# Expert weights held as two neighbouring rows per partition, with the matching operands' columns stepped by two

## The chip, the core and the metric

The kernel runs on one core of a Trainium2 chip. Its time is the device time of one execution in microseconds (us), the median of three runs. The engines that the text names are TensorE (PE, with its weight loads listed apart as PEld), VectorE (DVE), ScalarE (ACT), GpSimd (POOL) and SyncE (SP), whose queue issues nearly all loads. The core's 16 DMA engines move the bytes.

## What is computed

Two blocks of a network follow each other on 256 tokens of 1024 channels, all in float32. The first has a mixer (attention and a gated network), a norm, and then routed experts: each token goes to four of 32 experts. The change touches the experts alone; cut to what matters, the reference has for a group of tokens `xb` and an expert `e`:

```python
logits = (xt @ w_router + b_router).astype(jnp.float32)
top_vals, top_idx = lax.top_k(logits, TOP_K)
gates = jax.nn.softmax(top_vals, axis=-1).astype(x.dtype)
...
def expert_block(args):
    xb, e = args
    gt = jnp.minimum(xb @ w_gate[e] + b_gate[e], SWIGLU_LIMIT)
    up = jnp.clip(xb @ w_up[e] + b_up[e], -SWIGLU_LIMIT, SWIGLU_LIMIT)
    hid = gt * jax.nn.sigmoid(SWIGLU_ALPHA * gt) * (up + 1.0)
    return hid @ w_down[e] + b_down[e]
...
out = jnp.zeros((T + 1, D), x.dtype).at[row_tok].add(y_rows * row_gate[:, None])[:T]
```

Every expert has three matrices of 1024 x 1024 in float32, 4 MiB each, and all of them are read once: 384 MiB. The second block (another mixer and a network with a convolution) follows.

## The kernel before

**The experts' weights.** Each matrix is cut into four pieces of 256 rows, 1 MiB, that lie in memory in one stretch. `expert_pieces` lists them in the order of need: gate and up of expert e, then down of expert e-1. A piece lands in a tile of [128 partitions, 2048 floats]. Row 128 * k + p of the piece goes to half k of partition p, so a partition holds two rows that are 128 rows apart, each a run of 4 KB. `fetch` issues the DMAs on SP's queue (line 188, in `piece`); the first 18 pieces are issued in the first part (line 1251, in `pump`). There are 18 slots, used in turn: a piece can be issued when the products on the one that is 18 pieces ahead of it in its slot are done.

**The products.** Every expert has 64 slots for its tokens. For a pair of experts `gather` multiplies the tokens' rows `h` (as stationary operand, 128 columns at a time) with a matrix of zeros and ones: `xg` then holds, for each chunk k of 128 channels, the channels by partition and the slots by column. `product` sums over the chunks k: `xg[:, k]` is the stationary operand and half k % 2 of piece k // 2 is the moving one, so channel and weight row must agree in each partition. `hidden_t` turns the hidden values `sg` in four transposes to `hidT`, which plays the same part for the down product. `scatter` adds the results to the tokens' sums.

**The order.** It is written out by hand in the loop over experts at the end of `moe`: gate and up of e, the gather for the next pair (in every second e), down of e-1, the transposes. Behind expert 15 (`REST`) stands a loop, `overflow`, for experts with more than 64 tokens; its count is read at run time. It has weight loads of its own, [128, 1024], in the tile `wx`. `self.mm` is line 77 and `self.tr` line 81 for all products and transposes, so the groups of the profile are told apart by their tiles: `g`, `u`, `y` for the products with gate, up and down; `tr` and `sc` with `oh,h` for the gather; `tr<-ident,sg` for the transposes of `hidden_t`.

Of the kernel before, what the change touches and what calls it, by code (L numbers as in the profile page):

```python
# [30 lines left out]
# slots for pieces of weights: what each holds in the first part (raw pieces, their parts, the rest)  # L31
SLOTS_A = "r8 c1 c0 c2 c3 c4".split()
SLOTS_B = "r0 r1 r2 r3 r4 r5 r6 r7 h0 h1 h2 h3".split()
# the expert before whose successor the tokens that found no slot have their turn
# [25 lines left out]
class Net:  # L60
# [22 lines left out]
    def rsqrt_steps(self, pool, v, n, add=0.0, mul=1.0, floor=None, out=None):  # L83
        """Steps of 1/sqrt(max(mul * v, floor) + add) of small float32 tiles [128, n], by Newton steps from an
        integer guess. Halving and negating, as the steps want it, keeps the bits but for exponent and sign."""
# [26 lines left out]
    @staticmethod  # L112
    def alternate(*chains):
        """Emits chains of steps in turn, so that none waits for its own last step alone."""
        todo = list(chains)
        while todo:
            for g in list(todo):
                if next(g, todo) is todo:
                    todo.remove(g)
# [7 lines left out]
    def run(self):  # L127
# [20 lines left out]
        # for the experts' routing: ones; what comes before, in bits; the slots' numbers  # L148
# [33 lines left out]
    def piece(self, src, name="w"):  # L182
        """One weight piece: src is a list of (view of the tile, dram ap)."""
        pool, i = self.rings[self.turn % len(self.rings)]
        self.turn += 1
        t = pool.tile([128, 2048], F32, tag=i, name=self.nm(name))
        for view, ap in src(t):
            self.nc.sync.dma_start(view, ap)
        return t

    def front(self, fctx):
# [18 lines left out]
        # slots for weights: pieces as they come, their two parts, and what the output projection no longer needs  # L210
# [15 lines left out]
        # inputs, in the order in which they are needed; then the first experts' weights  # L226
# [8 lines left out]
        def add(src, *keys):  # L235
            """A piece and its halves, of columns for two keys, else of rows."""
            k, n = src.shape[1] , src.shape[2]
            spec.append((k, src))
            for x, key in enumerate(keys * (2 if len(keys) == 1 else 1)):
                halves.append((key, len(spec) - 1, (lambda t, x=x: t[:, :, x * n // 2:(x + 1) * n // 2]) if len(keys) == 2  # L240
                               else (lambda t, x=x: t[:, x * k // 2:(x + 1) * k // 2, :])))
# [49 lines left out]
        # masks  # L291
# [12 lines left out]
        # identities below one another  # L304
# [33 lines left out]
        def through(*names):  # L338
            """These slots go on to the experts' weights."""
            self.raw_slots += [slot[i] for i in names]  # L340
            self.pump()

        def channels(key):
            """[channel, token] of 128 columns."""
# [7 lines left out]
        # k transposed (each kv head in both halves), v by tokens, q transposed  # L352
# [8 lines left out]
        # spatial weights transposed  # L361
# [16 lines left out]
        # scores: groups of (query tile, chunks), each with one bank for either head of the chunks  # L378
# [39 lines left out]
        def trp(i):  # L418
            """Transposed, over what it came from."""
# [20 lines left out]
        # gated mlp: its second part by tokens  # L440
# [71 lines left out]
        # output projection, residual, layer norm, router  # L512
        wr, ln1g, ln1b = L["wr"], L["ln1g"], L["ln1b"]
        lst = [f2.tile([128, 4, 6], F32, tag="lst", name=self.nm("lst")) for _ in range(NT)]
        # the row that the norm's bias adds to the logits
        def by_experts(rhs, n, E):
            """[(part of the sum, expert), n] of the router's products."""
# [19 lines left out]
        def norm(t):  # L537
            """Steps of the norm, up to the last factor and the bias, and of that factor."""
# [72 lines left out]
    def split_biases(self, bf):  # L611
        """Biases of gate and up in three bf16 parts that add up to them exactly, by expert; in steps."""
# [13 lines left out]

    def expert_pieces(self):
        """The experts' weights as they are needed: gate and up, then down of the expert before."""
        r = []
        for e in range(NE + 1):  # L630
            for x, names in ((e, ("w_gate", "w_up")), (e - 1, ("w_down",)), (e, ("w_down",))):
                if x in range(NE) and (len(names) == 2 or (x == e) == (x == REST)):
                    for nme in names:
                        v = self.a[nme][0, x].rearrange("(k p) c -> p k c", p=128)
                        r += [((x, nme, i), v[:, 2 * i:2 * i + 2, :]) for i in range(4)]
        return r

    def fetch(self, n):
        """Loads the experts' weights up to the n-th piece."""
# [4 lines left out]
    def moe(self, mctx):  # L644
# [52 lines left out]
        def gather(b):  # L697
            xg[b] = m2.tile([128, KC, EB * CAP], F32, tag="xg", bufs=1, name=self.nm("xg"))
            for c0 in range(0, KC, 4):
                p = bank(*(("sc", 2) if c0 else ("tr", 1)), [128, 4, EB * CAP])  # L700
                for c in range(4):
                    for t in range(NT):
                        self.mm(p[:, c, :], self.h[:, t, (c0 + c) * 128:(c0 + c + 1) * 128],
# [7 lines left out]
        def scatter(yv, og_t, rows=128, sums=None):  # L711
            """With sums, these start with the sum so far and are left as they are."""
# [10 lines left out]
        def product(p, lhs, w, start):  # L723
            """p[(half, token)] (+)= lhs(k) @ w(k), either half of the columns in a half of the array."""
# [5 lines left out]
        def gated_slots(og, n):  # L730
            """[(expert, slot), token] of the gates of the slots' tokens."""
# [7 lines left out]
        def gates_of(b):  # L739
            """The gates in their slots; then, as a step of its own, turned."""  # L740
# [16 lines left out]
        def hidden_t(sg):  # L757
            hidT = m2.tile([128, 4, 2, CAP], F32, tag="hidT", bufs=1, name=self.nm("hidT"))
            p = bank("tr", 1, [128, 4, 128])
            for j in range(4):  # L760
                self.tr(p[:, j, :], sg[:, j * 128:(j + 1) * 128])
# [23 lines left out]
        def flush(sums=None):  # L785
            """Adds the last pair's products to the sum."""
# [3 lines left out]
        # experts with more tokens than slots: the rest, in further groups of slots  # L790
# [5 lines left out]
        def overflow_lists():  # L796
            """Entry i: the i-th group of slots past the first that some expert needs."""
# [24 lines left out]
            # first slot of the group: CAP * (1 + (entry - expert) / NE)  # L822
# [19 lines left out]
        def overflow():  # L842
            n = nc.values_load(lists["num"][0:1, 0:1], min_val=0, max_val=NL - 1)
            with tc.For_i(0, n, 1) as i:
# [15 lines left out]
                for k in range(KC):  # L860
                    for t in range(NT):
                        self.mm(p[:, k, :], self.h[:, t, k * 128:(k + 1) * 128], oh[:, t], start=t == 0, stop=t == NT - 1)
                nc.vector.tensor_copy(xo, p)

                def weights(nme):
                    def f(k):
                        w = m2.tile([128, D], F32, tag="wx", bufs=1, name=self.nm("wx"))
                        nc.sync.dma_start(w, a[nme][0, bass.ds(e, 1), k * 128:(k + 1) * 128, :].rearrange("o p c -> (o p) c"))
# [27 lines left out]
        def start_sum():  # L896
            # residual and the gated biases of the last product start the sum
# [17 lines left out]
        def ahead(n):  # L915
            """Before the work on the next n pieces: those that their forerunners have left slots for."""
# [44 lines left out]
        # the last sums start from what there is  # L961
# [5 lines left out]
        # the norms' weights, in slots that are through; the first weights of the mixer; then the last sums  # L967
# [15 lines left out]

    def late_consts(self, scratch):
        """Small inputs and tables of the second block; what only their making needs lies in scratch."""
# [15 lines left out]
        # vectors by channel: rows of 128, transposed later  # L1001
# [30 lines left out]
        # masks  # L1032
# [28 lines left out]
        # sine and cosine of the positions' angles  # L1061
# [9 lines left out]
    def late_tables(self):  # L1071
# [43 lines left out]
        # odd quarter turns swap the two; signs by the second bit  # L1115
# [29 lines left out]
    def diagonal(self, t, rs):  # L1145
        """rs on the diagonal: the right operand of a transposition that scales rows by it."""
        self.nc.vector.tensor_scalar(self.diag[:, t, :], self.ident, rs, None, op0=OP.mult)

    def tail_norm(self, sums):
        """x2 = layer_norm(sums); h = x2 * g of the next norm; diag = 1 / rms of x2. The steps of the two tiles  # L1150
        alternate."""
# [35 lines left out]
    # Weights of the second block, loaded in the order of use as slots come free. Every half of a piece is cut  # L1187
    # into two parts that add up to it exactly and that one pass of the tensor engine carries each; the product
    # of the low parts alone, below the rounding of the sums, stays out.
# [3 lines left out]
    def stream(self):  # L1193
# [6 lines left out]
        def by_k(key, w, c0, n, k):  # L1200
            """Pieces of k chunks of rows, halved by rows."""
# [38 lines left out]
    def pump(self):  # L1240
        """Loads as many pieces, and cuts as many halves, as there are slots for."""
# [27 lines left out]
    def parts(self, key, i=0):  # L1269
        """Both parts of the i-th half from now."""  # L1270
# [9 lines left out]
    def product(self, out, lhs, rhs, start, stop):  # L1280
        """out (+)= the product of the sums of the parts."""
# [3 lines left out]
    def warm(self, p, src, n):  # L1285
        """Products of no use, from when src is there: the tensor engine's clock falls when it has nothing to do."""
# [3 lines left out]
    def transposed_parts(self, src, dst, bank, order, between={}):  # L1290
        """dst[0] + dst[1] = src, its rows scaled by diag, transposed; order: (tile, first chunk)."""
# [11 lines left out]
    def mixer2(self, tctx):  # L1303
# [32 lines left out]
        # rwkv projections by channel, with the token shift  # L1336
        z, zl = big("z", (12, T)), big("zl")

        def rproj(nme, j0, chunks, tags, mid={}):
            """mid: what to put between the quarters of the sums."""  # L1340
# [89 lines left out]
        # decays to the ends of the chunks of 64  # L1430
# [11 lines left out]
        # projections of the attention  # L1442
# [6 lines left out]
        def tproj(nme, evict, lhs=hpt, nh=4, tag="pj"):  # L1449
            """Steps of a product by tokens."""  # L1450
# [29 lines left out]
        # products of keys and queries of the time mix: first those to be inverted, for all tokens  # L1480
# [11 lines left out]
        # inverses of the 16 x 16 blocks on the diagonal, one block to a partition  # L1492
# [13 lines left out]
        # by tokens  # L1506
# [43 lines left out]
        # norms and rotations of the attention's queries and keys  # L1550
# [102 lines left out]
        # gates of the branches  # L1653
# [9 lines left out]
        # group norm, bonus and gate of the time mix's output  # L1663
# [64 lines left out]
        # chunked time mix, one tile of 128 tokens (two chunks of 64) after the other  # L1728
        ST = {}
        yo = AW[:, :, :, 0, :]  # L1730
        for t in range(NT):
# [12 lines left out]
            # W = A_ak V  # L1744
# [4 lines left out]
            # inverses of blocks of 32, then of 64  # L1749
# [22 lines left out]
            # T [A | W]  # L1772
# [7 lines left out]
            # Q^T = R^T + (T A)^T A_rb^T  # L1780
# [6 lines left out]
            # transitions of the two chunks  # L1787
# [102 lines left out]
        # the second half of the last product, one tile after the other  # L1890
        for t in range(NT):
# [10 lines left out]
            # 1 / rms of the rows  # L1902
# [10 lines left out]
    def ffn2(self):  # L1913
        """The convolution's network."""
# [82 lines left out]
```

## Time and profile before

| | |
|---|---|
| three timed runs | 1591.0, 1594.75, 1597.09 us; median 1594.75 us |
| span of the profiled execution, from first to last instruction | 1592.6 us |
| own time of the profiled execution | not listed apart from its span; the median stands 2.15 us above it |
| TensorE busy | 1425.8 us, 90% |
| VectorE, ScalarE, GpSimd busy | 601.7, 363.8, 177.4 us |
| bytes moved by DMA | 491.14 MB, mean 308 GB/s |

Busy time is summed over the span, which has stages of very different kinds: the first mixer until about 115 us, the experts until about 1088 us, the second block behind them. A share of the whole span says little of any of them. "GB/s" is what the DMA engines moved in a stretch, "DMA share" the mean share of it in which they had a packet in work; it can pass 1 since the packets of one engine overlap a little.

### The profile page before, as it was taken

What the parts mean: (1) busy time and instruction counts of PE and PEld (TensorE: products, weight loads), DVE (VectorE), ACT (ScalarE), POOL (GpSimd) and SP (SyncE); (2) the same over time, 40 slices, a digit from 0 to 9 for tenths busy, and PEclk for the clock granted to TensorE, in tenths of its full rate; (3) what the DMA queues carried; (4) which work ended last, traced back from release to release, by engine and by line L of the source; (5) the groups of instructions that cost most, each with busy time, mean ns of one, the idle gap of its engine ahead of it and who ended that gap; (6) DMA issues with size and microseconds to landing.
All of it is one profiled execution on the core that took longest, in us unless ns stands there. A gap on an engine that the chain in (4) does not pass through costs nothing. (4 is left out here: it accounts for less than half of the span.)

```text
span 1592.6 us, 19400 instructions
## 1 busy us (share of the span) xinstructions
PE 1425.8 (90%) x7904; PEld 814.9 (51%) x7904; DVE 601.7 (38%) x1087; ACT 363.8 (23%) x607; POOL 177.4 (11%) x155
## 2 busy tenths in 40 slices
PE   8779999999898965998998988987998899999998
PEld 7663333333233212333332332324876787799998
DVE  5872122121121110121223211215578546876664
ACT  5441100101001000001010001002634223355552
POOL 4630000000000002000000000003444214200000
PEclk9988999999999987999999999998999999999999
DMA  9787999999999998999999999994433124665540
GB/s 303 277 316 310 409 408 409 409 409 409 409 409 409 409 409 313 410 409 409 409 409 409 409 409 409 409 409 172 159 113 116 31 76 153 210 234 183 193 151 27
DMA packets 168432, 491.14 MB, mean 308 GB/s; under 512 B 16392, under 2 KB 46792, under 8 KB 168341
## 3 DMA queue, kind: packets, MB, share of 16 engines
q1 hardware_dynamic: 167456, 489.02, 79.8%
q8 instruction: 63, 1.03, 0.3%
q0 software_dynamic: 512, 0.20, 0.1%
q10 hardware_dynamic: 372, 0.66, 0.1%
q14 instruction: 29, 0.23, 0.0%
HBM read 488.34 MB, written 1.51 MB: 308 GB/s over the span
## 5 line engine op out<-in xcount | busy, mean ns | idle before, releaser
L77 PE MATMUL g<-w,xg 128*64 128x512 f32 x1024 | 241.5, 620 | 12.5 <-DMA w<-in_w_gate_dram 12.5
L77 PE MATMUL u<-w,xg 128*64 128x512 f32 x1024 | 230.0, 595 | 15.9 <-DMA w<-in_w_up_dram 15.9
L77 PE MATMUL y<-w,hidT 128*64 128x512 f32 x1024 | 229.6, 596 | 7.6 <-DMA w<-in_w_down_dram 6.3
L1264 DVE TENSOR_TENSOR wp<-w,wp 128x1024 fp32r<-128x1024 f32 x115 | 154.0, 1364 | 102.4 <-ACT wp L1263 102.2
L1263 ACT CAST wp<-w 128x1024 fp32r<-128x1024 f32 (+1 forms) x148 | 151.6, 1037 | 168.0 <-PE pj L77 64.1
L77 PEld LDWEIGHTS g<-w,xg 128*64 128x64 f32 x1024 | 73.1, 143 | 160.0 <-issue 126.2
L77 PEld LDWEIGHTS u<-w,xg 128*64 128x64 f32 x1024 | 69.5, 137 | 166.4 <-issue 124.0
L77 PEld LDWEIGHTS y<-w,hidT 128*64 128x64 f32 x1024 | 69.8, 137 | 161.2 <-issue 134.2
L1264 POOL TENSOR_TENSOR wp<-w,wp 128x1024 fp32r<-128x1024 f32 (+1 forms) x33 | 78.5, 2385 | 587.2 <-ACT wp L1263 585.2
L770 ACT COPY y<-y 64x512 f32<-64x512 f32 x64 | 37.1, 579 | 378.4 <-PE y L77 377.9
L750 DVE TENSOR_SCALAR g<-g 128x512 f32<-128x512 f32 x32 | 22.1, 691 | 235.6 <-PE g L77 235.6
L763 DVE COPY hidT<-tr 128x256 f32<-128x256 f32 x32 | 13.6, 424 | 238.5 <-ACT hidT L762 238.5
L753 DVE TENSOR_SCALAR g<-u 128x512 f32<-128x512 f32 x32 | 22.1, 691 | 177.9 <-PE u L77 177.9
L77 PE MATMUL pj<-wp,h2p 128*128 128x512 f32 x336 | 85.3, 411 | 3.3 <-DVE wp L1264 3.2
L751 ACT ACTIVATE sg<-g 128x512 f32<-128x512 f32 x32 | 20.2, 630 | 260.3 <-DVE g L750 260.2
L77 PEld LDWEIGHTS pj<-wp,h2p 128*128 128x128 f32 x336 | 64.5, 196 | 20.4 <-DVE wp L1264 4.0
L77 PE MATMUL a<-h3p,wp 128*128 128x256 f32 x528 | 66.9, 283 | 0.5 <-DVE h3p L1299 0.5
L77 PEld LDWEIGHTS a<-h3p,wp 128*128 128x128 f32 x528 | 66.0, 191 | 2.2 <-DVE h3p L1299 0.7
L77 PE MATMUL b<-h3p,wp 128*128 128x256 f32 x528 | 66.9, 283 | 0.0
L77 PEld LDWEIGHTS b<-h3p,wp 128*128 128x128 f32 x528 | 64.9, 192 | 0.0
L77 PE MATMUL sc<-y,ogT 128*128 128x512 f32 x124 | 62.5, 619 | 2.5 <-ACT y L770 1.4
L77 PE MATMUL tr<-oh,h 128*128 128x128 f32 x256 | 36.0, 299 | 31.0 <-DVE oh L693 31.0
(527 smaller groups left out, 1591.9 us busy)
## 6 DMA issues: line engine op xcount, KB each, us to landing
w<-in_w_gate_dram SPq DMA_DIRECT2D x128, 1024.0 KB, 18.5
w<-in_w_up_dram SPq DMA_DIRECT2D x128, 1024.0 KB, 18.5
w<-in_w_down_dram SPq DMA_DIRECT2D x128, 1024.0 KB, 18.5
w<-in_w_in_dram SPq DMA_DIRECT2D x27, 1024.0 KB, 5.0
w<-in_w_ffn_up_dram SPq DMA_DIRECT2D x22, 1024.0 KB, 5.3
w<-in_w_ffn_down_dram SPq DMA_DIRECT2D x11, 1024.0 KB, 7.5
w<-in_w_out_dram SPq DMA_DIRECT2D x8, 1024.0 KB, 8.1
w<-in_w_branch_b_dram SPq DMA_DIRECT2D x2, 1024.0 KB, 4.9
```

The lines of the kernel that those rows point to most:

```text
L77: return self.nc.tensor.matmul(out, lhsT, rhs, start=start, stop=stop)
L750: nc.vector.tensor_scalar(g1, pg, 7.0, None, op0=OP.min)
L751: nc.scalar.activation(sg, g1, AF.Sigmoid, scale=1.702)
L753: nc.vector.tensor_scalar(g1, pu, -7.0, 7.0, op0=OP.max, op1=OP.min)
L763: nc.vector.tensor_copy(hidT[:, 2:4].rearrange("p j f s -> p j (f s)"), p[:, 2:4])
L770: nc.scalar.copy(yv[64 * i:64 * i + 64, hf * 512:(hf + 1) * 512], py[64 * hf:64 * hf + 64, :])
L1263: nc.scalar.copy(t[:, 0], src)
L1264: self.low[j % len(self.low)].tensor_tensor(t[:, 1], src, t[:, 0].bitcast(F32), op=OP.subtract)
```

## The change

A piece is still 256 neighbouring rows. Now row 2p + x of it goes to half x of partition p: a partition holds two neighbouring rows, which are one run of 8 KB in memory. What stands in half x of piece i is then no longer channels 128k to 128k + 127 but every second channel of 256, from 256i + x. The operands that are multiplied with it must hold the same channels, so the columns of `h` and `sg` that are taken for chunk k are stepped by two (`pairs`); the loads in the overflow loop take every second row likewise. The rest of the diff removes comments, and the lines behind `split_biases` stand 7 or 8 lines further down.

```diff
+    @staticmethod
+    def pairs(k):
+        i, x = divmod(k, 2)
+        return slice(256 * i + x, 256 * i + 256, 2)
...
-                        v = self.a[nme][0, x].rearrange("(k p) c -> p k c", p=128)
-                        r += [((x, nme, i), v[:, 2 * i:2 * i + 2, :]) for i in range(4)]
+                        v = self.a[nme][0, x].rearrange("(i p x) c -> i p x c", p=128, x=2)
+                        r += [((x, nme, i), v[i]) for i in range(4)]
...
-                        self.mm(p[:, c, :], self.h[:, t, (c0 + c) * 128:(c0 + c + 1) * 128],
+                        self.mm(p[:, c, :], self.h[:, t, self.pairs(c0 + c)],
                                 oh[b][:, t].rearrange("p e s -> p (e s)"), start=t == 0, stop=t == NT - 1)
...
-                self.tr(p[:, j, :], sg[:, j * 128:(j + 1) * 128])
+                self.tr(p[:, j, :], sg[:, self.pairs(j)])
...
-                        self.mm(p[:, k, :], self.h[:, t, k * 128:(k + 1) * 128], oh[:, t], start=t == 0, stop=t == NT - 1)
+                        self.mm(p[:, k, :], self.h[:, t, self.pairs(k)], oh[:, t], start=t == 0, stop=t == NT - 1)
...
-                        nc.sync.dma_start(w, a[nme][0, bass.ds(e, 1), k * 128:(k + 1) * 128, :].rearrange("o p c -> (o p) c"))
+                        rows = a[nme][0, bass.ds(e, 1)].rearrange("o (i p x) c -> i x (o p) c", p=128, x=2)
+                        nc.sync.dma_start(w, rows[k // 2, k % 2])
```

No instruction moves: on every engine the same instructions stand in the same order. On SP's queue the experts' loads have another form. Before, in the loop over experts, with the piece's tile, its source and the shape of the destination as the instruction carries it (partitions, halves, floats of a run):

```order
200 L188 DMA w_2831<-in_w_up_dram 128x2x1024
201 L188 DMA w_2833<-in_w_up_dram 128x2x1024
202 L188 DMA w_2835<-in_w_down_dram 128x2x1024
203 L188 DMA w_2837<-in_w_down_dram 128x2x1024
204 L188 DMA w_2839<-in_w_down_dram 128x2x1024
```

With the change the same five rows are:

```order
200 L188 DMA w_2831<-in_w_up_dram 128x2048
201 L188 DMA w_2833<-in_w_up_dram 128x2048
202 L188 DMA w_2835<-in_w_down_dram 128x2048
203 L188 DMA w_2837<-in_w_down_dram 128x2048
204 L188 DMA w_2839<-in_w_down_dram 128x2048
```

The two runs of 1024 floats per partition have become one of 2048; place, order and size of the loads are as they were.

## Rows read from the trace of the kernel before

**Rows 1.** The page: span, and busy time of each engine.

```profile
span 1592.6 us, 19400 instructions
...
PE 1425.8 (90%) x7904; PEld 814.9 (51%) x7904; DVE 601.7 (38%) x1087; ACT 363.8 (23%) x607; POOL 177.4 (11%) x155
```

**Rows 2.** Windows: busy PE, PEld, DVE, ACT, POOL; clock, DMA share, GB/s.

```profile
150.00:580.00 430.00, 398.74 (x1870) 144.96 (x1868) 79.76 (x146) 40.59 (x82) 2.26 (x4) 0.98 1.03 409
...
620.00:1061.00 441.00, 401.11 (x1890) 145.07 (x1889) 86.37 (x185) 41.34 (x85) 6.61 (x31) 0.99 1.03 407
1061.00:1088.00 27.00, 26.06 (x97) 9.13 (x98) 5.22 (x9) 3.79 (x7) 0.35 (x1) 1.00 0.96 378
1088.00:1592.00 504.00, 465.67 (x3218) 414.48 (x3216) 329.98 (x553) 214.91 (x326) 105.85 (x64) 0.97 0.40 135
```

**Rows 3.** The DMA view: packets, queues, and one kind of issue with its landing.

```profile
DMA packets 168432, 491.14 MB, mean 308 GB/s; under 512 B 16392, under 2 KB 46792, under 8 KB 168341
...
q1 hardware_dynamic: 167456, 489.02, 79.8%
q8 instruction: 63, 1.03, 0.3%
...
w<-in_w_gate_dram SPq DMA_DIRECT2D x128, 1024.0 KB, 18.5
```

**Rows 4.** The DMA view of 10:13, 50:53 and 200:560 us, in this order.

```profile
DMA packets 1099, 1.11 MB, mean 370 GB/s; under 512 B 16, under 2 KB 1099, under 8 KB 1099
...
DMA packets 584, 1.16 MB, mean 388 GB/s; under 512 B 16, under 2 KB 16, under 8 KB 584
...
DMA packets 38244, 147.17 MB, mean 409 GB/s; under 512 B 2340, under 2 KB 2340, under 8 KB 38228
```

**Rows 5.** TensorE's waits for weights: 110:600 us, then 600:1062 (us, times, longest).

```profile
PE u L77 <- DMA w<-in_w_up_dram: 6.8, 12, 0.6
PE g L77 <- DMA w<-in_w_gate_dram: 5.4, 9, 0.6
...
PE y L77 <- DMA w<-in_w_down_dram: 1.8, 4, 0.6
...
PE u L77 <- DMA w<-in_w_up_dram: 9.1, 16, 0.6
PE g L77 <- DMA w<-in_w_gate_dram: 7.2, 12, 0.6
PE y L77 <- DMA w<-in_w_down_dram: 4.5, 8, 0.6
```

**Rows 6.** TensorE's timeline in both stretches: start, us, operation, [idle before <-releaser].

```profile
415.06 1.94 PE L77 MATMUL y<-w,hidT 128*64 128x512 f32 x8 [0.62 <-DMA w<-in_w_down_dram]
...
579.45 1.94 PE L77 MATMUL y<-w,hidT 128*64 128x512 f32 x8 [0.31 <-DMA w<-in_w_down_dram]
...
689.95 0.66 PE L81 MATMUL tr<-ident,sg 128*128 128x128 f32 x4
...
704.82 2.05 PE L77 MATMUL tr<-oh,h 128*128 128x128 f32 x16
...
708.49 4.11 PE L77 MATMUL sc<-y,ogT 128*128 128x512 f32 x8
...
722.81 7.03 PE L77 MATMUL g<-w,xg 128*64 128x512 f32 x32
...
743.72 0.66 PE L81 MATMUL tr<-ident,sg 128*128 128x128 f32 x4
...
925.46 1.94 PE L77 MATMUL g<-w,xg 128*64 128x512 f32 x8 [0.62 <-DMA w<-in_w_gate_dram]
928.02 1.94 PE L77 MATMUL g<-w,xg 128*64 128x512 f32 x8 [0.62 <-DMA w<-in_w_gate_dram]
...
1061.06 1.94 PE L77 MATMUL u<-w,xg 128*64 128x512 f32 x8 [0.63 <-DMA w<-in_w_up_dram]
```

**Rows 7.** SP's waits, 580:625 us.

```profile
SPq L844 <- SPq L844: 17.2, 7, 2.6
```

## The prediction

> **What bounds the kernel now.** I read the page first and then cut the span into stages. The span is 1592.6 us and TensorE is busy for 90% of it, the DMA queue for 80% [rows 1, 3], so the whole-span shares cannot say which of the two sets the end. The table by stage can: from 150 to 580 us and again from 620 to 1061 us the loads run at 409 and 407 GB/s with the DMA share at 1.03, with no slack, while TensorE is busy for 399 of 430 and 401 of 441 us [rows 2]. These two stretches are the routed experts. Behind them stands 1088 to 1592 us at 135 GB/s, the second block, which TensorE bounds [rows 2].
>
> That a flat 409 GB/s is a limit of the loads and not the pace of a consumer is seen in two views. TensorE waits for weights, 25 times in the first stretch and 36 in the second, 14.0 and 20.8 us in sum [rows 5]. And the timeline tells when it keeps up by itself: a pair of experts without a wait takes 743.72 - 689.95 = 53.8 us, while 24 pieces of 1 MiB at 409 GB/s take 24 x 2.563 = 61.5 us [rows 6, 4]. So TensorE starts each stretch with a backlog of landed pieces, works it off at 7.7 us per pair, and from 415.06 us (first wait) to the end of the stretch it stands at the loads: 2.56 us from one piece to the next, of which 0.62 idle [rows 6]. Each piece lands 18.5 us after its issue, that is some seven pieces' time [rows 3]: the queue never runs dry there, whatever SP waits for. The end of each stretch is therefore its start plus pieces x 2.56 us.
>
> **The change part by part.** The number, bytes and order of the DMAs stay the same, and so does the order on every engine; what changes is that a piece, now two runs of 4 KB per partition, becomes one of 8 KB. So everything hangs on the price of a run. No 8 KB run is in the trace: nearly all packets are under 8 KB (168341 of 168432), and the 63 packets of the instruction queue, 1.03 MB, show only that larger packets exist [rows 3]. But three stretches have one run length each: 1 KB runs move 370 GB/s, 2 KB runs 388, 4 KB runs 409 [rows 4]. With 16 DMA engines busy, the time of one packet on its engine is 16 x bytes / rate: 44.3, 84.5 and 160.2 ns. If a packet costs a fixed time plus bytes, the fixed part is twice the shorter packet less the longer one: 88.6 - 84.5 = 4.1 ns from the first two, 168.9 - 160.2 = 8.7 ns from the last two. One 8 KB run in place of two of 4 KB saves one fixed part, so it takes 311.7 ns by the second figure (420 GB/s) and 316.3 by the first (414).
>
> I take 8.7 ns, from the rows nearest in length and from the stretch that the change acts in. A piece has 16 packets on each engine and will have 8, so it saves 8 x 8.7 = 0.070 us: 2.563 becomes 2.493 us. Below, the bound is nothing (runs that are cut at 4 KB again); above, I let the figure grow as it grew from 4.1 to 8.7, to 13.3 ns, 0.106 us per piece.
>
> [...]
>
> Now the pieces that this is multiplied with. First stretch: 430 us at 409 GB/s are 168 pieces, and it ends with a down weight that TensorE waits for at 579.45 us [rows 2, 6]: 168 x 0.070 = 11.8 us. Second stretch: 441 us at 407 GB/s are 171 pieces, up to the last up weight, awaited at 1061.06 us [rows 2, 6]: 12.0 us. Between them lies the branch for overflowing experts. SP waits there 17.2 us, seven times up to 2.6 us, for its own pieces in flight [rows 7], TensorE idles over it and then goes on. These seven drain faster too: 7 x 0.070 = 0.5 us. Sum: 24.3 us.
>
> Can TensorE take that? A piece for which it waits costs 2.56 us, a piece in a train 7.03/4 = 1.76 [rows 6]; so each 0.62 us of idle gives back 0.80 us. The 14.0 and 20.8 us of waits are worth 18 and 27 us, and 11.8 and 12.0 fit in. The loads stay the bound: 24 x 2.493 = 59.8 us per pair against 53.8.
>
> What I cost at nothing. The pieces loaded before 150 us land sooner, but TensorE waits for none of them: its first wait for a weight comes at 415.06 us [rows 6]. Without that cover it would be worth 18 pieces x 0.070 = 1.3 us. SP waits for slots as before, with seven pieces in flight as cover; a faster load that meets a full ring only waits longer for its slot. From 1061 us on TensorE needs 27 us for the last two down products and the sums, and the eight down pieces behind the last up piece take 20.5 us, now 19.9; that chain and the 504 us behind it shift as they are [rows 2]. The body of the overflow branch has the same number of 4 KB runs, and no load of its weights is among the issues.
>
> The other edit makes the columns that TensorE loads as its stationary operand step by two: 512 gather products and 128 transposes, 40 per pair. No row before has such a step. The 32 gather products of a pair take 708.49 - 704.82 = 3.67 us, 115 ns each [rows 6]. Bounds: nothing, or a doubling to 230 ns. At nothing they vanish; at the doubling see the rival below. I take nothing, since any price under 20 ns (640 x 20 ns = 13 us, within what TensorE has left over, 45 - 24 = 21 us, and 320 x 20 ns = 6.4 us against 18 - 11.8 = 6.2 in the tighter first stretch) is hidden in the waits.
>
> **The sum.** Against the profiled execution: 1592.6 - 24.3 = 1568.3 us of span. The median of the runs lies 2.15 us above that span, and I let that stand: 1594.75 - 24.3 = 1570.5 us.
>
> **The rivals.** *A small fixed cost.* The engines are held by the bytes, and a run costs only the 4.1 ns of the 1 and 2 KB rows. For it: three points do not lie on one line, so a constant is my reading; against it: the larger figure is the nearer one. 339 x 8 x 4.1 ns = 11.1 us, with the drain 11.4: 1583.4 us. [...]
>
> *The change does not reach the engines.* The 8 KB run is cut into two packets of 4 KB, or the memory itself gives no more than 409 GB/s. For it: the rate of the 4 KB rows is flat to within 1 GB/s over hundreds of microseconds, as a ceiling would be, and no packet of the weights' queue is longer. Against it: a ceiling on bytes would leave the packet price to vanish at 4 KB, and it grew instead. Then nothing moves: 1594.75 us. [...]
>
> *Slower: the stepped columns hold up TensorE.* If a stationary load with a step of two takes twice as long, each of the 640 products costs 115 ns more, 36.8 us in either stretch. The waits give back 18 and 27 us of it; the rest, 18.8 and 9.8 us, is lost and TensorE becomes the bound: 1594.75 + 28.6 = 1623 us. The gain starts to shrink from 20 ns per product in the first stretch and is gone where 640 products eat 45 us, at 70 ns. For it speaks that at 115 ns the loads and products of the gather follow each other without a wait between them, so nothing would cover a longer load; against it, that neither number nor size of the loads changes, and that a doubling is the far end of what I can bound. [...]
>
> **How the numbers follow.** The forecast holds 0.66: 8.7 ns, between 1557 (13.3 ns: 339 x 0.106 + 0.7 = 37 us, where the first stretch's 17.9 us just meets TensorE's 18) and some 1580. The small cost has 0.14, no effect 0.11, the stepped columns 0.06, and 0.03 I leave to an order of addresses that the memory likes less, which no row prices. The range goes from 1557 to 1590: it holds the first two cases and leaves out the last three, 0.20. One measurement of this kernel tells about 0.5%, 8 us, from no change. Faster by more than that: 0.66 + 0.12 of the small cost = 0.78. Within it: 0.11 + 0.02 = 0.13. Slower: 0.09.
>
> **What would show it.** The packets fall by 98304 (256 per piece become 128, in three times 128 pieces [rows 3]) to some 70000; if they do not, the run is cut. The table by stage shows about 420 GB/s in both expert stretches; 409 is the second rival, 414 the first. Pieces that TensorE waits for stand 2.49 us apart. Its first wait comes later than 415 us, since it wins only 6.0 us per pair, and its waits for weights fall from 35 to about 16 us. The gather products of a pair still take 3.67 us; 7 us there, with the waits for weights gone, is the slower rival. All of the gain lies before 1061 us, and the stage from there to the end keeps its length. The prediction fails if one of these lengths differs, above all the packet's.

## The result, and the profile after

The changed kernel takes 1568.73 us (median of 4 runs, 1567.13 to 1571.36) against 1594.84 us of the kernel before (4 runs, 1591.0 to 1597.09): a ratio of 0.9836, interval 0.9818 to 0.9854. That is 26.1 us less by the medians. The two profiled executions differ by 1592.6 - 1569.3 = 23.3 us of span; that of the changed kernel is the slowest of its four.

The page of the changed kernel, to be held against [rows 1, 3]:

```profile
span 1569.3 us, 19400 instructions
...
PE 1423.9 (91%) x7904; PEld 825.2 (53%) x7904; DVE 600.2 (38%) x1087; ACT 364.1 (23%) x607; POOL 177.6 (11%) x155
...
DMA packets 119279, 491.14 MB, mean 313 GB/s; under 512 B 16391, under 2 KB 46791, under 8 KB 70036
...
q1 hardware_dynamic: 118304, 489.02, 78.6%
```

Bytes and the number of instructions are the same. The packets fall from 168432 to 119279, by 49153, that is 384 pieces x 128 and one: each pair of 4 KB runs has become one packet. TensorE is busy for 1.9 us less than before and the kernel ends 23 us earlier, so what went was idle time.

The stretches of the experts in the table by stage (columns as in [rows 2]), and then the DMA view of 200:540 us:

```profile
150.00:570.00 420.00, 396.36 (x1870) 148.54 (x1868) 79.71 (x146) 40.60 (x82) 2.26 (x4) 0.99 1.01 418
620.00:1035.00 415.00, 390.40 (x1836) 146.23 (x1834) 85.57 (x183) 40.23 (x82) 0.00 (x0) 0.98 1.01 421
```

```profile
DMA packets 19748, 143.03 MB, mean 421 GB/s; under 512 B 2277, under 2 KB 2277, under 8 KB 2309
...
w<-in_w_gate_dram SPq DMA_DIRECT2D x44, 1024.0 KB, 19.8
```

The first stretch needs 420 us for what took 430 before (1870 products in both windows), at 418 and 421 GB/s where [rows 2] have 409 and 407; the first of the two still holds the ramp before 200 us (291 GB/s from 150 to 160 us). An 8 KB packet takes 16 x 8192 / 421 = 311.3 ns of its engine, two of 4 KB took 2 x 160.2 [rows 4].

TensorE's waits for weights, 110:1062 us (us, times, longest), and its timeline:

```profile
PE u L77 <- DMA w<-in_w_up_dram: 9.9, 20, 0.6
PE g L77 <- DMA w<-in_w_gate_dram: 4.8, 10, 0.6
PE y L77 <- DMA w<-in_w_down_dram: 0.9, 2, 0.4
```

```profile
118.98 3.75 PE L77 MATMUL tr<-oh,h 128*128 128x128 f32 x16 [0.94 <-DVE oh L700]
...
476.68 1.94 PE L77 MATMUL g<-w,xg 128*64 128x512 f32 x8 [0.31 <-DMA w<-in_w_gate_dram]
479.16 1.94 PE L77 MATMUL g<-w,xg 128*64 128x512 f32 x8 [0.54 <-DMA w<-in_w_gate_dram]
481.64 1.94 PE L77 MATMUL g<-w,xg 128*64 128x512 f32 x8 [0.55 <-DMA w<-in_w_gate_dram]
...
606.66 3.78 PE L77 MATMUL tr<-oh,h 128*128 128x128 f32 x16 [29.01 <-DVE oh L700]
...
696.98 2.15 PE L77 MATMUL tr<-oh,h 128*128 128x128 f32 x16
698.96 2.05 PE L77 MATMUL sc<-oh,h 128*128 128x128 f32 x16
700.85 4.12 PE L77 MATMUL sc<-y,ogT 128*128 128x512 f32 x8
...
1039.60 1.94 PE L77 MATMUL u<-w,xg 128*64 128x512 f32 x8 [0.56 <-DMA w<-in_w_up_dram]
```

61 waits of 34.8 us in sum [rows 5] have become 32 of 15.6 us. The first comes at 476.68 us, not at 415.06, since TensorE now works off its backlog of landed pieces more slowly; the pieces that it then waits for stand 2.48 us apart, not 2.56 [rows 6].

Three rows cut the kernel into its parts: the first gather product, the gather that waits behind the overflow branch (line 700 there is line 693 before), and the last up product that waits for its piece. The first two in the kernel before:

```profile
117.07 3.75 PE L77 MATMUL tr<-oh,h 128*128 128x128 f32 x16 [0.94 <-DVE oh L693]
...
615.96 3.57 PE L77 MATMUL tr<-oh,h 128*128 128x128 f32 x16 [30.01 <-DVE oh L693]
```

Subtracting the starts, and from the span's end the last of them (1061.06 us before, [rows 6]), gives the parts below; the other kernels' are from the same three rows of theirs.

| kernel (us) | first gather to the branch's end | from there to the last up | rest |
|---|---|---|---|
| before | 498.9 | 445.1 | 531.5 |
| changed | 487.7 | 432.9 | 529.7 |
| e1_cut_runs | 499.0 | 444.2 | 530.3 |
| e3_steps_only | 500.1 | 445.1 | 531.4 |
| e4_runs_only | 486.2 | 432.9 | 530.3 |
| e6_gate_up_only | 490.5 | 436.8 | 531.7 |

The change gains 11.2 and 12.2 us in the two stretches of the experts. The rest is 1.8 us shorter, though no edit reaches it. Kernels that load as before lie 1.2 us apart there (530.3 to 531.5), and e4, with the loads of the change, has 530.3; so most of the 1.8 us is spread, and for what is left no run shows a cause. The first gather starts 1.9 us later than before, which lies within the 115.65 to 119.05 us of the kernels run here.

### The profile page after: what moved, and what is told of

It is laid out like the page before. It is cut to its first block, busy times and chain, and to the rows that moved or that the text cites. A ratio compares the mean times of both kernels' runs of the same rounds, so it can differ in the third digit from the quotient of the medians.

```text
span 1569.3 us, 19400 instructions
## 1 busy us (share of the span) xinstructions
PE 1423.9 (91%) x7904; PEld 825.2 (53%) x7904; DVE 600.2 (38%) x1087; ACT 364.1 (23%) x607; POOL 177.6 (11%) x155
## 2 busy tenths in 40 slices
DMA packets 119279, 491.14 MB, mean 313 GB/s; under 512 B 16391, under 2 KB 46791, under 8 KB 70036
## 5 line engine op out<-in xcount | busy, mean ns | idle before, releaser
L770 DVE COPY hidT<-tr 128x256 f32<-128x256 f32 x32 | 13.6, 424 | 230.4 <-ACT hidT L769 230.4
L77 PEld LDWEIGHTS pj<-wp,h2p 128*128 128x128 f32 x336 | 62.8, 191 | 18.5 <-DVE wp L1272 2.7
## 6 DMA issues: line engine op xcount, KB each, us to landing
w<-in_w_gate_dram SPq DMA_DIRECT2D x128, 1024.0 KB, 19.8
w<-in_w_up_dram SPq DMA_DIRECT2D x128, 1024.0 KB, 19.8
w<-in_w_down_dram SPq DMA_DIRECT2D x128, 1024.0 KB, 19.8
```

Of the source, the lines that this page charges most:

```text
L77: return self.nc.tensor.matmul(out, lhsT, rhs, start=start, stop=stop)
L770: nc.vector.tensor_copy(hidT[:, 2:4].rearrange("p j f s -> p j (f s)"), p[:, 2:4])
```

## The experiments

The theory is the prediction's: a packet costs its DMA engine a fixed time of some 9 ns beside its bytes, so the length of a run is the whole gain. Against it stand three other explanations. The memory may like the new order of addresses, whatever the runs. The stepped columns may cost something that the gain hides. And the gain may be one of SP, whose DMA instructions have fewer runs to describe.

**e1_cut_runs.** The change, but the halves of a tile stand 16 bytes apart, so that a partition's two neighbouring rows are two runs again.

```diff
-        t = pool.tile([128, 2048], F32, tag=i, name=self.nm(name))
+        t = pool.tile([128, 2056], F32, tag=i, name=self.nm(name))
...
-            t = self.piece(lambda t: [(t.rearrange("p (k c) -> p k c", k=2), src)])
-            self.got[key] = t.rearrange("p (k c) -> p k c", k=2)
+            t = self.piece(lambda t: [(t.rearrange("p (k c) -> p k c", k=2)[:, :, 0:1024], src)])
+            self.got[key] = t.rearrange("p (k c) -> p k c", k=2)[:, :, 0:1024]
```

> Neighbouring rows as in the change, with the stepped columns, but the two halves of a piece's tile stand 16 bytes apart, so that a piece is two runs of 4 KB per partition again; the warm-up's zeros lie in another tile to make room. Theory A (each packet costs its DMA engine a fixed 9 ns, so fewer, longer packets are the whole gain): the packets are those of before, the expert stretches run at 409 GB/s, 1595 us. Rival B (the gain comes from reading neighbouring rows of memory, not from the length of the runs): 421 GB/s and 1569 us.

1592.85 us (10 runs), ratio to before 0.9984 (0.9972 to 0.9997). Its page, and then its DMA view of 200:540 us:

```profile
DMA packets 168431, 491.14 MB, mean 309 GB/s; under 512 B 16391, under 2 KB 46791, under 8 KB 168340
```

```profile
DMA packets 36232, 139.42 MB, mean 410 GB/s; under 512 B 2220, under 2 KB 2220, under 8 KB 36216
```

With the packets back, the rate is back at 410 GB/s and the time with it, though rows, order of addresses and stepped columns are those of the change. A packet thus ends where a run breaks on either side: in the kernel before it breaks in memory (168432 packets), here in the tile (168431). What the order of addresses may be worth is the 0.16% that is left, a tenth of the gain.

**e3_steps_only and e4_runs_only.** The first adds the stepped columns of `gather` and `hidden_t` to the kernel before; the second takes them out of the changed kernel:

```diff
-                        self.mm(p[:, c, :], self.h[:, t, self.pairs(c0 + c)],
+                        self.mm(p[:, c, :], self.h[:, t, (c0 + c) * 128:(c0 + c + 1) * 128],
...
-                self.tr(p[:, j, :], sg[:, self.pairs(j)])
+                self.tr(p[:, j, :], sg[:, j * 128:(j + 1) * 128])
```

> The loads of before (runs of 4 KB, rows 128 apart), with the columns of h and sg stepped by two: the products then sum over channels that do not belong together, so the output is not the reference's. Theory A: the steps cost TensorE 0.2 us per gather of a pair and some 0.08 us per four transposes, all of it hidden in its waits for weights: 1595 us, 409 GB/s. Rival C (the steps cost something at the end, which the faster loads of the change more than pay for): 1597 us or more.

> The runs of 8 KB of the change, with the unstepped columns of before: again channels that do not belong together, so the output is not the reference's. Theory A: 421 GB/s, the gathers back at 3.67 us, the time that of the change, 1569 us, since TensorE waits for weights at the end of each stretch either way. Rival C: 1567 us or less, by what the steps cost.

The steps alone: 1595.41 us (10 runs), ratio 1.0002 (0.9992 to 1.0011). The runs alone: 1568.76 us (4 runs), ratio 0.9828 (0.9811 to 0.9844), the time of the change to 0.03 us. The steps are not free, only hidden: the weight loads of the gather and of the transposes (count; ns min/median/max), in the kernel before and then in the changed one:

```profile
L77 PEld LDWEIGHTS tr<-oh,h x256: 186/192/338, 117.0 to 1003.2; 128*128 128x128 f32 x128
L81 PEld LDWEIGHTS tr<-ident,sg x128: 137/140/230, 143.5 to 1074.3; 128*128 128x128 f32 x128
```

```profile
L77 PEld LDWEIGHTS tr<-oh,h x256: 193/196/331, 118.9 to 983.6; 128*128 128x128 f32 x128
L81 PEld LDWEIGHTS tr<-ident,sg x128: 194/209/226, 145.5 to 1052.9; 128*128 128x128 f32 x128
```

A gather takes 700.85 - 696.98 = 3.87 us where it took 3.67 [rows 6], 6 ns more per product; the load of a transpose is 69 ns longer. The times of e3 and e4 hold nothing of that, so it goes into time that TensorE had to spare. Its waits for weights don't show the exchange itself: their sum is 35.8 us in e3 against 34.8 before, at a granted clock of 1.00 against 0.98 in 200:540 us, and 15.1 us in e4 against 15.6 in the change.

**e6_gate_up_only.** The gate and up pieces as in the change, the down pieces and the columns of `sg` as before: two thirds of the pieces.

```diff
-                        v = self.a[nme][0, x].rearrange("(i p x) c -> i p x c", p=128, x=2)
+                        if nme == "w_down":
+                            v = self.a[nme][0, x].rearrange("(i x p) c -> i p x c", p=128, x=2)
+                        else:
+                            v = self.a[nme][0, x].rearrange("(i p x) c -> i p x c", p=128, x=2)
...
-                self.tr(p[:, j, :], sg[:, self.pairs(j)])
+                self.tr(p[:, j, :], sg[:, j * 128:(j + 1) * 128])
```

> Gate and up weights as in the change with the stepped columns of h; down weights and the columns of sg as before. Theory A: a dose of two thirds: 256 of the 384 pieces have half the packets, 33000 fewer than with none changed would be half of 65536, so 65536 fewer than before, a mean of 417 GB/s in the expert stretches, 1595 - 2/3 x 26 = 1577.5 us. A rival by which the gain is one of SP's issuing (fewer descriptors per load let it keep eight pieces in flight instead of seven, however long they are) has the gain depend on the longest pieces alone, with no proportion: near 1595.

1579.96 us (4 runs), ratio 0.9899 (0.9882 to 0.9915). Its DMA view of 200:540 us:

```profile
DMA packets 25191, 141.69 MB, mean 417 GB/s; under 512 B 2252, under 2 KB 2252, under 8 KB 13548
```

And the packets of its page:

```profile
DMA packets 135663, 491.14 MB, mean 312 GB/s; under 512 B 16391, under 2 KB 46791, under 8 KB 102804
```

The medians give 14.6 us, a little less than two thirds of 26.1 (17.4), which lies in the interval (1594.59 times 0.0085 to 0.0118, 13.6 to 18.8 us). In the table of parts the second stretch, free of the start's chance, gives 8.3 of 12.2 us, 68%. The packets fall by 32768 (256 pieces x 128) from the 168431 of e1 and e3, two thirds of the 49152 of the change; the 65536 that I expected was a slip. The gain goes by the count of packets.

**e2_two_loads.** The change, with each of its pieces behind the first 18 issued as two DMAs of one row per partition: 128 runs of 4 KB in each, twice the DMA instructions.

```diff
-            self.nc.sync.dma_start(view, ap)
+            if len(view.shape) == 3:
+                for x in range(2):
+                    self.nc.sync.dma_start(view[:, x, :], ap[:, x, :])
+            else:
+                self.nc.sync.dma_start(view, ap)
```

> The change, with every piece behind the first 18 loaded by two DMAs of 512 KB, one for each half, so that each DMA has 128 packets of 4 KB, as many as a piece of the change has of 8 KB. Theory A (each packet costs its engine a fixed 9 ns): 409 GB/s, 1595 us, as before the change, though SP's DMAs are as small as in the change. Rival D (the gain lies in SP's issuing: a DMA with half the descriptors is issued sooner, and more are in flight): 421 GB/s or near, below 1580 us.

1593.52 us (10 runs), ratio 0.9988 (0.9978 to 0.9999). Its table by stage:

```profile
200.00:540.00 340.00, 322.47 (x1486) 118.31 (x1488) 66.27 (x124) 31.46 (x64) 2.26 (x4) 0.98 1.03 408
640.00:1020.00 380.00, 357.31 (x1656) 132.52 (x1654) 79.67 (x174) 36.56 (x76) 0.00 (x0) 0.98 1.03 409
```

Its SP, by the waits of 150:1061 us and by the timeline (the instruction stands in line 190 here):

```profile
SPq L190 <- DMA w<-in_w_down_dram: 205.7, 224, 1.7
```

```profile
337.21 0.33 SPq L190 DMA_DIRECT2D w<-in_w_down_dram  x1
```

Each DMA now has 128 runs, as one of the change has, and SP behaves as in the change (last section): an instruction takes 0.33 us, not the 2.31 of the kernel before, and waits for an earlier load. The rate is nevertheless that of 4 KB packets, and so is the time. What SP does is not where the gain is from. One thing e2 adds: each load brings 16 packets of under 512 B, so there are 22248 of them in place of 16391. They can't have eaten the gain. The same rates come out at 421 and 409 GB/s with loads of 1 MiB (change and before) and at 422 and 410 with loads of 4 MiB (e5, below), which have a quarter of these packets; by an estimate from these four rates, each known to a whole GB/s, one costs its engine at most 16 ns, and one more per piece and engine would leave 418 GB/s.

**e5_loads_alone.** The price by itself: SP loads whole matrices of 4 MiB one behind the other into four tiles, with runs of another length in each stretch, and the output is zeros; nothing else runs.

```diff
+                b = kb // 4
+                nc.sync.dma_start(v.rearrange("p (a r) -> p a r", a=8 // b),
+                                  w.rearrange("(a p b) c -> p a (b c)", p=128, b=b))
```

> Loads alone, nothing is computed and the output is zeros: matrices of 4 MiB one after the other in runs of 1, 2 and 4 KB, then 4 KB runs cut from neighbouring rows, then runs of 8, 16 and 32 KB, then 4 KB again. Theory A with its fixed 9 ns per packet of up to 32 KB: 409, 409, 421, 427, 430 and 409 GB/s from the first 4 KB runs on; 1 and 2 KB runs 353 and 388. Rival B (neighbouring rows): 421 already for the cut 4 KB runs. If the fixed price were paid once per some size between 8 and 32 KB (longer runs cut into packets by the hardware), the rate stays at 421 from that size on.

The DMA view of eight windows, with runs of 1, 2 and 4 KB, of 4 KB from neighbouring rows, of 8, 16 and 32 KB, and of 4 KB again:

```profile
DMA packets 31081, 31.34 MB, mean 348 GB/s; under 512 B 480, under 2 KB 31081, under 8 KB 31081
DMA packets 15351, 30.95 MB, mean 387 GB/s; under 512 B 240, under 2 KB 240, under 8 KB 15351
DMA packets 15737, 63.48 MB, mean 410 GB/s; under 512 B 240, under 2 KB 240, under 8 KB 15736
DMA packets 13304, 53.64 MB, mean 413 GB/s; under 512 B 208, under 2 KB 208, under 8 KB 13304
DMA packets 7967, 63.30 MB, mean 422 GB/s; under 512 B 240, under 2 KB 240, under 8 KB 240
DMA packets 2776, 42.86 MB, mean 429 GB/s; under 512 B 160, under 2 KB 160, under 8 KB 160
DMA packets 2230, 64.69 MB, mean 431 GB/s; under 512 B 256, under 2 KB 256, under 8 KB 256
DMA packets 5080, 20.48 MB, mean 410 GB/s; under 512 B 79, under 2 KB 79, under 8 KB 5080
```

16 x bytes / rate gives 47.1, 84.7, 159.8, 310.6, 611.1 and 1216 ns per run of 1, 2, 4, 8, 16 and 32 KB. Twice the shorter less the longer is the fixed part: 9.5, 9.6, 9.1, 10.1 and 6 ns. Rates in whole GB/s leave the last two uncertain by 1.5 and 2.8 ns, so one constant of 9 to 10 ns fits all but the last, and that nearly. Runs of 8 KB are one packet each (63.30 MB in 7727 packets above the small ones), and so are those of 16 and 32 KB: 42.86 MB in 2616 and 64.69 MB in 1974 packets are 16384 and 32771 bytes in the mean. Neighbouring rows without longer runs move 413 against 410 GB/s: as in e1, at most a small part of the gain is theirs.

**e7_step_four.** Where the slower rival begins: the changed kernel with columns stepped by four, the step that runs of 16 KB would need.

```diff
-        i, x = divmod(k, 2)
-        return slice(256 * i + x, 256 * i + 256, 2)
+        i, x = divmod(k, 4)
+        return slice(512 * i + x, 512 * i + 512, 4)
```

> The change with the columns of h and sg stepped by four in place of two; the channels then do not belong together and the output is not the reference's. It measures what the step itself costs TensorE. By theory A only the products of the gather and the transposes may slow down. If the step by four costs no more than the step by two: 3.9 us per gather, 1569 us. [...]

1586.06 us (4 runs), ratio to before 0.9939 (0.9919 to 0.9959): 17.3 us above the change. TensorE's timeline at a gather, then its weight loads (the third row is the gather's other half), then its longest wait of 600:1062 us, the one behind the overflow branch:

```profile
704.55 4.00 PE L77 MATMUL tr<-oh,h 128*128 128x128 f32 x16
...
712.12 4.12 PE L77 MATMUL sc<-y,ogT 128*128 128x512 f32 x8
```

```profile
L77 PEld LDWEIGHTS tr<-oh,h x256: 307/329/332, 117.4 to 1002.7; 128*128 128x128 f32 x128
L81 PEld LDWEIGHTS tr<-ident,sg x128: 195/212/222, 144.9 to 1068.5; 128*128 128x128 f32 x128
...
L77 PEld LDWEIGHTS sc<-oh,h x256: 329/329/330, 121.1 to 1006.4; 128*128 128x128 f32 x128
```

```profile
PE tr L77 <- DVE oh L700: 15.9, 1, 15.9
```

The gather takes 712.12 - 704.55 = 7.57 us, 237 ns per product: 116 more than at a step of two, the doubling of the rival. In neither stretch does TensorE wait for a weight any more, though the loads run at 419 and 421 GB/s: a pair now takes it 58.4 us (the mean of three, 649.10 to 824.29 us) against 59.5 us for 24 pieces, so its backlog of landed pieces lasts to the end of each stretch and TensorE sets that end.

Not every gather costs 3.7 us more. The gather behind the branch, in the change and then in e7 (columns as in [rows 2]):

```profile
606.60:613.00 6.40, 6.27 (x32) 6.08 (x32) 0.46 (x3) 0.37 (x1) 6.24 (x14) 0.60 0.42 139
```

```profile
609.00:617.00 8.00, 7.73 (x32) 7.54 (x32) 0.60 (x3) 0.37 (x1) 7.63 (x20) 0.75 0.53 190
```

Behind its long wait (29.0 and 15.9 us) TensorE's granted clock is partly at the lower of the two levels that the trace shows (single us of the change read 0.50 until 611 us and 1.00 from 612 us; the means of the two windows are 0.60 and 0.75). There a gather takes 6.27 us at a step of two and 7.73 at four, 1.5 more; its weight loads at a step of four take 329 ns at either level, as the weight loads above show (307 to 332 over all of them), while those at a step of two take up to 331 ns there and 196 else (medians of the change). The first gather is alike: 5.99 and 7.63 us. The account: 14 x 3.7 + 1.5 + 1.6 = 55 us more. Of it the 32 waits give back at most 32 x (2.48 - 1.76) = 23 us, and the wait behind the branch, shorter by 29.0 - 15.9, another 13. That leaves some 19 us where 17.3 were measured. My estimate, with 115 ns more (a gather product's time, [rows 6]) in each of a pair's 40 products, was 4.6 us per pair and 1569 to 1575 us: it had counted the work but let the waits pay for nearly all of it.

Runs of 16 KB in the whole kernel were not tried: they need pieces of 2 MiB and another ring of slots, and by this run the gather would have to find its columns without a step of four.

## Why the prediction was right

The forecast was 1570.5 us and the time is 1568.73. The 24.3 us of gain that it adds up stand between two measures: the parts of the profiled executions give 11.2 + 12.2 = 23.4 us in the experts' stretches, the medians 26.1. That the medians come so close is in part chance, since single runs of the change lie 4 us apart. Step by step:

- *What bounds.* The loads do, in both stretches. e1 keeps all else but the tile's width and takes the packets back, and the rate and time are those of before; e2, with twice as many DMAs, says the same.
- *The fixed part, 8.7 ns.* In the kernel 2 x 160.2 - 311.3 = 9.1 ns, alone 9.1 as well; 421 GB/s for a forecast 420, 2.48 us per piece for 2.493.
- *The two stretches, 11.8 and 12.0 us.* 11.2 (12.7 in e4) and 12.2 us.
- *The drain at the branch, 0.5 us.* It didn't come. The wait was 17.2 us in seven parts [rows 7] and is 18.3 in eight (below): each load is done sooner, but there is one more of them. What it expected of SP, waits for slots as before, did not come either (last section); the time doesn't show it.
- *TensorE can take it.* Its waits fell to 15.6 us (forecast 16). The stepped columns were put at nothing, with the gather to stay at 3.67 us; it takes 3.87. They cost 6 ns per gather product and 20 ns per transpose, whose four take 0.74 us where they took 0.66: together 512 x 6 + 128 x 20 ns = 5.6 us of TensorE's time, 9 ns on the mean of the 640, under the 20 ns that the waits could hide. e3 and e4 find it nowhere in the total. The 53.8 us per pair was one spacing; three pairs from gather to gather (653.41 to 816.65 us before) take 54.4 on the mean, which changes no term of the sum.
- *Nothing behind 1061 us.* 529.7 against 531.5 us, of which spread explains most (table of parts).

Two lines of the prediction were wrong without moving its sum. Packets were to fall by 98304 to some 70000; 256 less 128 in 384 pieces is 49152, and 119279 are left, of which 70036 are under 8 KB. And the 4.1 ns of the small-cost rival came from a 3 us window of 1 KB runs at 370 GB/s [rows 4]; over 90 us such runs move 348, and their fixed part is 9.5 ns. So rows of the kind that it was taken from refute it.

That the change doesn't reach the engines falls by the packet count. The slower rival falls at a step of two (121 ns per product, not 230) and is real at four, at the size that it named. There it still left the kernel 9 us faster than before: its point of no gain, 45 us of added work, missed the slack behind the branch, 13 us, and that the gathers at the lower clock cost less; the rest of the distance is not traced. The gather's weight load takes 196 ns at a step of two, 4 more than before, and 329 at four, 137 more; that of a transpose takes 209 at two, 69 more, and 212 at four, hardly more than at two.

## What to carry to other kernels

In a stretch that the loads bound, count packets: here each cost its DMA engine some 9 ns on top of its bytes (9.1 in the kernel; 9.1 to 10.1 alone, from 1 to 16 KB), so giving a partition neighbouring rows (409 to 421 GB/s from 4 KB to 8 KB) is worth the count of packets saved x 9 ns / 16. Then look for what pays for the operand that must follow: a column step of two cost 6 ns per product and hid in time that TensorE had to spare, a step of four cost 116 ns and made TensorE the bound.

## What the runs showed of the hardware

**More loads in flight, and another wait of SP.** A piece lands 19.8 us after its issue instead of 18.5 [rows 3], though it moves faster: 19.8 / 2.48 = 8.0 pieces in flight, where there were 18.5 / 2.56 = 7.2. SP's longest waits in the experts' stretches, before (the longest of several alike) and after (us, times, longest):

```profile
SPq L188 <- PE y L77: 147.1, 72, 5.2
```

```profile
SPq L188 <- DMA w<-in_w_down_dram: 198.7, 97, 2.5
SPq L188 <- DMA w<-in_w_up_dram: 197.6, 98, 2.3
SPq L188 <- DMA w<-in_w_gate_dram: 194.4, 93, 3.7
...
SPq L851 <- SPq L851: 18.3, 8, 2.5
```

It waited mainly for products to free a slot; now it waits mainly, 288 times, for an earlier load. Its DMA instructions change with it. Those for up weights, with ns min/median/max, first of the kernel before (the pieces that are issued ahead, then those of the loop over experts), then of the changed one, and below them one load of e5 with 256 runs of 16 KB:

```profile
L1251 SPq DMA_DIRECT2D w<-in_w_up_dram x8: 367/368/420, 57.8 to 102.9; - x8
...
L188 SPq DMA_DIRECT2D w<-in_w_up_dram x120: 367/2306/4754, 135.3 to 1042.9; - x120
```

```profile
L188 SPq DMA_DIRECT2D w<-in_w_up_dram x120: 327/328/407, 137.7 to 1019.7; - x120
```

```profile
868.48 0.37 SPq L88 DMA_DIRECT2D r<-in_w_down_dram  x1
```

In the loop of the kernel before, an instruction with 256 runs holds SP for 2.31 us in the median, nearly a piece's time; with 128 runs it is gone in 0.33 us, of 8 KB in the change and of 4 KB in e2. The count of runs in a DMA doesn't set that alone: with the same 256 runs the pieces that are issued ahead take 0.37 us, and so does the load of e5, where four loads are in flight at most. So the 2.31 us are for the most part a wait within the instruction while some seven loads of 256 runs are in flight; for what it waits no run shows. In e2 a load lands after 10.2 us, again 8 times the 1.28 us that half a piece takes. What sets the eight is not shown by a run either.

**The rate without packets.** With 9.1 ns taken off, an 8 KB packet leaves 16 x 8192 / (310.6 - 9.1) = 435 GB/s for the bytes, an estimate, and the 32 KB runs come to 431. What an engine does in the 9 ns of a packet no run shows.

**The transposes and a step of four.** The gather's weight loads go from 196 to 329 ns from step two to step four, and the 329 ns are the same at either level of the clock (e7); those of the transposes stay at 209 and 212. No run here shows why.
